# Residual rows of four token tiles loaded ahead of the last product, into the large pool instead of a ring of two

## The chip, the cores and the metric

The kernel runs on one core of a Trainium2 chip. The metric is the device time of one execution in microseconds (us), lower is better. A core has five engines that take instructions in program order, each from its own queue: TensorE (PE), VectorE (DVE), ScalarE (ACT), GpSimd (POOL) and SyncE (SP). SP computes nothing here. It issues nearly all the loads and stores (DMAs), again in program order, and an issue that has to wait holds back everything behind it in SP's queue.

## What is computed

1024 tokens of width 1024, all in float32, pass through two blocks. The three places that the change touches have one shape: a wide hidden activation is multiplied by a "down" matrix and added to the residual row of the token.

```python
# first block
z = rms_norm(h, norm_mlp_g);   h = h + square(relu(z @ w_up)) @ w_down        # way back 1
z = rms_norm(h, norm_ple_g);   h = h + sigmoid(z @ w_ple_gate + b) * (p @ w_ple_proj)
h = rms_norm(h, norm_final_g)
# second block: ffn with a gate, then a mixer, then ffn with a gate
h = h + 0.5 * rms(ffn1(h)) * g1      # ffn(z) = (silu(z @ w_g) * (z @ w_u)) @ w_o    # way back 2
h = h + rms(mixer(h)) * g2
h = h + 0.5 * rms(ffn2(h)) * g3                                                # way back 3
```

## The kernel before

The tokens are cut into eight tiles of 128 rows, t = 0 to 7. A float32 product is made of three matmuls on split operands: ACT rounds an operand to its high half (`wh` of the activation, `tt` of the weight; L687), DVE subtracts to get the low half (`wl`, and the second `tt`; L688), and PE multiplies high by high, high by low and low by high.

`down_s` is the way back. It forms the product with `w_down` (or `f_out`) by seven products of half-size blocks, as Strassen does, in the order 2, 1, 5, 3, 6, 7, 4. Each product is a row of units. A unit loads one piece of the activation from memory (`sd`, from `hs`) and one of the weight (`wd`, from the weight itself, or `td`, a prepared difference), both issued by SP at L660 into tiles of the large pool `u`, of 4 KB a partition. The units of a product are numbered q = 0, 1, and so on. The first way back has the loads `wd`, and DVE subtracts two of them (L669) before the split; the second and third have `td`.

At the end of a product its four PSUM banks are emptied into `Y`, by copies on ACT (L730) or by additions on DVE (L731). After product 7 come four additions for the tiles 4 to 7, and product 4 then finishes these four tiles. For each finished tile `first(t)` is called: it loads the residual row (`xr`, 512 KB, L307) through a pool of two buffers, the ring, and so the loads of the tiles 6 and 7 have to wait until the rows of the tiles 4 and 5 have been used. In the second and third ways back the residual row is used at L1128 (`Y = Y * r + xr`), after a multiplication by the gain (L1121) and after `r`, the reciprocal root that POOL makes of a row's sum of squares (L383, L384). The result goes out by a DMA at L1130, from ACT's queue in way back 2 (to `xb`), from SP's in way back 3 (to `out`). In way back 2 `xs` (L128, ACT) is the normalized tile that PE transposes (L155) for the next projection.

The order of the instructions on each engine is made ahead of time by a scheduler that simulates the program; dependences added by `after` steer it and cost nothing on the chip. "Stage 1, 2 and 3" below are the ends of the three ways back: the last part of product 7, product 4, and what follows until the next product starts. They lie at about 924 to 990 us, 1757 to 1830 us and 2997 to 3054 us.

Of the kernel before, what the change touches and what calls it, by code (L numbers as in the profile page):

```python
# [21 lines left out]
NT = S // P  # L22
# [90 lines left out]
class Z:  # L113
# [5 lines left out]
    def __init__(self, m, gain, whole=False, early=False):  # L119

        self.m, self.gain, self.whole, self.early = m, gain, whole, early
        self.src, self.left = [None] * NT, [0, 1]
        self.tiles = [[], []]
        self.drain = None
# [123 lines left out]
class Model:  # L248
    def __init__(self, ctx, tc, a, out):
        self.tc, self.nc, self.a, self.out = tc, tc.nc, a, out  # L250
        pool = lambda n, b, **k: ctx.enter_context(tc.tile_pool(name=n, bufs=b, **k))
        self.pc = pool("c", 1)
        self.pu = pool("u", 32)
        self.pw = pool("w", NW)
        self.pr = pool("r", 2)
        self.pt = pool("t", 5)
        self.psm = pool("sm", 8)
        self.pd = pool("d", 1, space=DRAM)
        self.last_raw = None
        self.ps = pool("ps", 8, space=PSUM)  # L260


# [363 lines left out]
    def rights(self, w, tw, d):  # L626
# [9 lines left out]
        for i, t in enumerate((x, y)):  # L636
            nc.sync.dma_start(out=tw[d // 2][2 * i : 2 * i + 2, d % 2].rearrange("i p f -> p i f"), in_=t)


    RIGHT = {5: 0, 7: 1, 4: 2, 6: 3}  # L640


    LEFT = {2: (0, 0), 1: (0, 1), 5: (1, 0), 3: (1, 1), 6: (2, 0), 7: (2, 1), 4: (3, 0)}

    def down_s(self, hs, w, Y, done, z=None, aside={}, tail=1, tw=None):

        nc = self.nc
# [4 lines left out]
        ends = [self.late]  # L654
# [36 lines left out]
        def unit(p, q):  # L691
            n = qs[q][1]
            g, i = self.LEFT[p]
            s = load("sd", hs[q][g][i, :n], q)
            return pair(("wh", "wl"), s, n), pair(("u", "u"), right(p, q), n)

        def mm(bank, un, c, t, start, stop):
            (sh, sl), (th, tl) = un
            ts = slice(t * P, (t + 1) * P)
            for k, (x, y) in enumerate(((sh, th), (sh, tl), (sl, th))):  # L700
                self.mark = nc.tensor.matmul(bank, x[:, c, ts], y[:, c], start=start and k == 0, stop=stop and k == 2,  # L701
                                             skip_group_check=True)

        def product(p, banks, start, out, mid=None):
            nq = len(qs)
            head = nq - (tail if p == 4 else 1)
            for q in range(head):
                un = unit(p, q)
                for c in range(qs[q][1]):
                    for t in range(4):  # L710
                        mm(banks[t], un, c, t, start and q == 0 and c == 0, False)
                ends.append(self.mark)
                for f in aside.get((p, q), ()):
                    f()
                if q % 2 and chores:
                    chores.pop(0)()
            uns = [(q, unit(p, q)) for q in range(head, nq)]
            if mid:
                mid()
            for t in range(4):  # L720
                for q, un in uns:
                    for c in range(qs[q][1]):
                        mm(banks[t], un, c, t, start and q == 0 and c == 0, q == nq - 1 and c == qs[q][1] - 1)
                out(t)
            ends.append(self.mark)
# [31 lines left out]
        if z:  # L757
            chores.append(lambda: z.flush(3))
        product(7, a, False, lambda t: plus(4 + t, B, a[t]))

        def rest():
            while chores:
                chores.pop(0)()
            if z:
                z.ready(0)
# [201 lines left out]
    def mlp(self, z, aside={}):  # L967
        nc = self.nc
        hs, xy = [], {}

        def use(n, quarter, bank, other):
            i, j = quarter
            if (n, j) not in xy:
                xy[n, j] = self.u("h", shape=[P, 2, H], tag="s" if (n, j) == (1, 1) else "u")
            o = xy[n, j][:, (1 - i) if j == 0 else i]
            if other is not None:
                nc.vector.tensor_tensor(o, bank, other, op=ALU.add)
                bank = o
            nc.scalar.activation(o, bank, AF.Relu)
            nc.scalar.activation(o, o, AF.Square)  # L980
            if quarter == (1, 0):
                self.lay_by(hs, n, xy.pop((n, 0)), xy.pop((n, 1)), "s")

        self.ups_s(z, use)
        Y = [None] * NT

        def first(t):
            r = self.raw(self.xm[t], name="xr", tag="xr", after=self.mark)
            nc.vector.tensor_tensor(Y[t], Y[t], r, op=ALU.add)
            return self.rstd(Y[t])  # L990

        done, z = self.follow("norm_ple_g", first, lambda t, r: (Y[t], r))
        aside = dict(aside)
        aside[7, 4] = [self.ple_in]
        self.down_s(hs, self.a["w_down"], Y, done, z, aside)
        self.resume()
        return Y, z

# [115 lines left out]
    def seam(self, Y, G, xin, xout, gain, whole=False):  # L1114

        nc = self.nc

        def first(t):
            x = self.raw(xin[t], name="xr", tag="xr", after=self.mark)
            r = self.rstd(Y[t])  # L1120
            nc.vector.tensor_tensor(Y[t], Y[t], G, op=ALU.mult)  # L1121
            return x, r

        def second(t, s):
            if s is None:
                return
            x, r = s
            nc.vector.scalar_tensor_tensor(out=Y[t], in0=Y[t], scalar=r, in1=x, op0=ALU.mult, op1=ALU.add)  # L1128
            r = self.rstd(Y[t]) if gain else None
            (nc.scalar if gain else nc.sync).dma_start(out=xout[t], in_=Y[t])  # L1130
            return r

        if gain:
            return self.follow(gain, first, second, lambda t, r: (Y[t], r), whole=whole)
        state = []

        def done(t):
            state.append(first(t))
            if t:
                second(t - 1, state[t - 1])  # L1140
            if t in (3, NT - 1):
                second(t, state[t])
                state[t] = None

        return done, None

    def ffn(self, n, z, seam, aside={}):
        nc = self.nc
        hs, G, X = [], {}, {}

        def use(p, quarter, bank, other):
            d, up = divmod(p, 2)
            i, j = quarter
            at = (1 - i) if j == 0 else i
            T = X if up else G
            if (d, j) not in T:
                T[d, j] = self.u("h", shape=[P, 2, H]) if up else self.u("g", tag="s", shape=[P, 2, H])
            o = T[d, j][:, at]
            if other is not None:
                nc.vector.tensor_tensor(o, bank, other, op=ALU.add)  # L1160
                bank = o
            if not up:
                nc.scalar.activation(o, bank, AF.Silu)
                return
            nc.vector.tensor_tensor(o, bank, G[d, j][:, at], op=ALU.mult)  # L1165
            if quarter == (1, 0):
                self.lay_by(hs, d, X.pop((d, 0)), X.pop((d, 1)), "u")

        w, tw = self.a["f%d_out" % n], []

        def also(k, of):
            if (k + 1) * w.shape[1] // of > k * w.shape[1] // of:
                self.rights(w, tw, k * w.shape[1] // of)

        self.ups_s(z, use, also)
        Y = [None] * NT
        done, z = seam(Y)
        self.down_s(hs, w, Y, done, z, aside, 1 if z else 2, tw)
        return z

    def half_scale(self, row, name):
# [505 lines left out]
    def block2(self, z, aside):  # L1687
        x0, x1, x2 = self.xd, self.spill("xb"), self.spill("xc")
        rows = [self.out[t * P : (t + 1) * P, :] for t in range(NT)]
        G1 = self.half_scale(2, "g1")  # L1690
        z = self.ffn(1, z, lambda Y: self.seam(Y, G1, x0, x1, "mix_pre_g_2", True), aside)
        self.resume()
        G2 = self.bcast(self.a["rows"][3], "g2")
        z = self.mixer2(z, lambda Y: self.seam(Y, G2, x1, x2, "ffn2_pre_g_2", None))
        G3 = self.half_scale(4, "g3")
        self.ffn(2, z, lambda Y: self.seam(Y, G3, x2, rows, None))

def build(tc, a, out):
    with ExitStack() as ctx:
# [30 lines left out]
```

## Time and profile before

| what | value |
|---|---|
| median of three runs | 3056.68 us (3054.08 to 3061.38) |
| the profiled execution, its own time | 3056.01 us |
| its span in the profile | 3054.2 us |
| PE busy | 2828.5 us (93%) |
| DVE, ACT, POOL busy | 1797.1 us (59%), 1320.1 us (43%), 784.1 us (26%) |
| mean granted clock of PE | 0.968 |
| loads `sd` in all | 126 of 512 KB, median 5.5 us from issue to landing |

The span is the time between the first and the last instruction that the profiler recorded; 1.8 us of the execution's own time lie around it. A share of busy time is a mean over the whole span. What a change in one stage is worth is read from that stage's own waits.

### The profile page before, as it was taken

What the parts mean: (1) busy time and instruction counts of PE and PEld (TensorE: products, weight loads), DVE (VectorE), ACT (ScalarE), POOL (GpSimd) and SP (SyncE); (2) the same over time, 40 slices, a digit from 0 to 9 for tenths busy, and PEclk for the clock granted to TensorE, in tenths of its full rate; (3) what the DMA queues carried; (4) which work ended last, traced back from release to release, by engine and by line L of the source; (5) the groups of instructions that cost most, each with busy time, mean ns of one, the idle gap of its engine ahead of it and who ended that gap; (6) DMA issues with size and microseconds to landing.
All of it is one profiled execution on the core that took longest, in us unless ns stands there. A gap on an engine that the chain in (4) does not pass through costs nothing. (4 is left out here: it accounts for less than half of the span.)

```text
span 3054.2 us, 33886 instructions
## 1 busy us (share of the span) xinstructions
PE 2828.5 (93%) x12585; PEld 2303.4 (75%) x12585; DVE 1797.1 (59%) x2561; ACT 1320.1 (43%) x1921; POOL 784.1 (26%) x626
## 2 busy tenths in 40 slices
PE   8998999989979989999989999997789999998997
PEld 7777877767757867778777878886677778777776
DVE  4586655575767366666667561417735756565445
ACT  5446554442335473323324362236655533332343
POOL 3320222200211221111122041349854112111001
PEclk9999999999989999999999999999899899999999
DMA  4114344474466123454466562423113244446645
GB/s 145 57 47 138 131 145 152 156 259 160 166 233 220 56 90 106 153 164 151 164 222 237 207 222 81 155 83 111 42 49 131 87 152 159 159 153 207 225 160 200
DMA packets 198200, 452.93 MB, mean 148 GB/s; under 512 B 20533, under 2 KB 25233, under 8 KB 198033
## 3 DMA queue, kind: packets, MB, share of 16 engines
q1 hardware_dynamic: 193424, 433.97, 41.9%
q10 hardware_dynamic: 4608, 16.78, 1.4%
q8 instruction: 99, 1.62, 0.2%
q14 instruction: 69, 0.56, 0.1%
HBM read 316.51 MB, written 129.99 MB: 146 GB/s over the span
## 5 line engine op out<-in xcount | busy, mean ns | idle before, releaser
L701 PE MATMUL b<-tt,wh 128*128 128x512 f32 x2128 | 686.2, 403 | 74.0 <-ACT tt L687 64.4
L541 PE MATMUL b<-zh,wh 128*128 128x512 f32 x1680 | 646.9, 398 | 35.4 <-ACT wh L481 25.6
L541 PE MATMUL b<-zh,wl 128*128 128x512 f32 x1680 | 625.3, 393 | 4.5 <-ACT wl L511 4.0
L541 PE MATMUL b<-zl,wh 128*128 128x512 f32 x1560 | 615.2, 395 | 8.4 <-DVE zl L211 8.4
L701 PEld LDWEIGHTS b<-tt,wh 128*128 128x128 f32 x2128 | 409.3, 194 | 181.5 <-ACT tt L687 73.8
L701 PE MATMUL b<-tt,wl 128*128 128x512 f32 x1064 | 424.1, 399 | 0.0
L541 PEld LDWEIGHTS b<-zh,wh 128*128 128x128 f32 x1680 | 319.8, 191 | 123.9 <-ACT wh L481 38.8
L541 PEld LDWEIGHTS b<-zh,wl 128*128 128x128 f32 x1680 | 318.2, 190 | 75.5 <-ACT wl L511 6.7
L541 PEld LDWEIGHTS b<-zl,wh 128*128 128x128 f32 x1560 | 296.4, 190 | 73.9 <-DVE zl L211 13.4
L688 DVE TENSOR_TENSOR wl<-sd,wh 128x1024 fp32r<-128x1024 f32 x140 | 167.6, 1197 | 190.3 <-ACT wh L687 190.3
L482 POOL TENSOR_TENSOR wl<-raw,wh 128x1024 fp32r<-128x1024 f32 x51 | 123.3, 2418 | 526.1 <-ACT wh L481 486.6
L701 PEld LDWEIGHTS b<-tt,wl 128*128 128x128 f32 x1064 | 206.7, 194 | 43.6
L481 ACT ACTIVATE wh<-raw 128x1024 fp32r<-128x1024 f32 x120 | 127.2, 1060 | 238.4 <-DMA raw<-in_f_in 95.2
L352 POOL TENSOR_TENSOR wl<-raw,wh 128x1024 fp32r<-128x1024 f32 (+1 forms) x58 | 142.7, 2465 | 322.0 <-ACT wh L351 290.2
L687 ACT ACTIVATE wh<-sd 128x1024 fp32r<-128x1024 f32 x140 | 141.5, 1011 | 154.6 <-DMA sd<-hs 111.9
L383 POOL TENSOR_SCALAR v<-ss 128x1 f32<-128x1 f32 x80 | 47.9, 599 | 472.5 <-ACT junk L376 466.3
L619 POOL TENSOR_TENSOR hw<-h 128x512 f32<-128x512 f32 x38 | 60.2, 1583 | 421.1 <-DVE h L1165 188.1
L687 ACT ACTIVATE tt<-wd 128x1024 fp32r<-128x1024 f32 x92 | 94.6, 1028 | 150.3 <-DVE wd L669 133.1
L505 DVE TENSOR_TENSOR s<-raw 128x512 f32<-128x512 f32 x60 | 82.2, 1370 | 107.5 <-DMA raw<-in_f_in 100.6
L482 DVE TENSOR_TENSOR wl<-raw,wh 128x1024 fp32r<-128x1024 f32 x69 | 88.7, 1286 | 84.2 <-ACT wh L481 43.2
L351 ACT ACTIVATE wh<-raw 128x1024 fp32r<-128x1024 f32 (+1 forms) x58 | 59.5, 1031 | 168.2 <-issue 42.7
L688 DVE TENSOR_TENSOR tt<-wd,tt 128x1024 fp32r<-128x1024 f32 x92 | 110.2, 1198 | 27.6 <-ACT tt L687 26.8
(358 smaller groups left out, 5003.4 us busy)
## 6 DMA issues: line engine op xcount, KB each, us to landing
sd<-hs SPq DMA_DIRECT2D x126, 512.0 KB, 5.5
raw<-in_f_in SPq DMA_DIRECT2D x94, 512.0 KB, 3.7
wd<-in_w_down SPq DMA_DIRECT2D x64, 512.0 KB, 6.3
raw<-in_f_out SPq DMA_DIRECT2D x44, 512.0 KB, 3.6
tw<-raw SPq DMA_DIRECT2D x44, 512.0 KB, 2.9
td<-tw SPq DMA_DIRECT2D x40, 512.0 KB, 6.3
hs<-h SPq DMA_DIRECT2D x38, 512.0 KB, 3.1
hs<-hw SPq DMA_DIRECT2D x38, 512.0 KB, 3.0
```

The costliest lines, as they stand in the source:

```text
L351: nc.scalar.activation(h, r, AF.Copy)
L352: nc.gpsimd.tensor_tensor(l, r, h.bitcast(F32), op=ALU.subtract)
L383: nc.gpsimd.tensor_scalar(out=v, in0=ss, scalar1=1.0 / D, scalar2=EPS, op0=ALU.mult, op1=ALU.add)
L481: nc.scalar.activation(hi.rearrange("p a b -> p (a b)"), x, AF.Copy)
L482: eng.tensor_tensor(lo.rearrange("p a b -> p (a b)"), x, hi.bitcast(F32).rearrange("p a b -> p (a b)"), op=ALU.subtract)
L505: v.tensor_tensor(s1, a21, a22, op=ALU.add)
L541: self.mark = nc.tensor.matmul(bank, w, x, start=start and k == 0 and i == 0, stop=k == 3 and i == 2, skip_group_check=True)
L619: g.tensor_tensor(wt[:, 1], x[:, 1], y[:, 0], op=ALU.subtract)
L687: nc.scalar.activation(hi[:, :n], x[:, :n], AF.Copy)
L688: v.tensor_tensor(lo[:, :n], x[:, :n], hi.bitcast(F32)[:, :n], op=ALU.subtract)
L701: self.mark = nc.tensor.matmul(bank, x[:, c, ts], y[:, c], start=start and k == 0, stop=stop and k == 2, skip_group_check=True)
```

## The change

After the last addition of product 7 has been emitted, four loads `xe` are issued on SP, one for each residual row of the tiles 4 to 7, into tiles of the pool `u`. `row` then hands these tiles to `first(t)`, and only the tiles 0 to 3 still go through the ring.

```diff
+    def row(self, xin, t):
+        return self.rows.pop(t) if t in self.rows else self.raw(xin[t], name="xr", tag="xr", after=self.mark)
...
         product(7, a, False, lambda t: plus(4 + t, B, a[t]))
+        for t in range(4, NT):
+            x = self.rows[t] = self.u("xe")
+            self.after(nc.sync.dma_start(out=x, in_=xin[t]), ends[-5])
...
         def first(t):
-            r = self.raw(self.xm[t], name="xr", tag="xr", after=self.mark)
+            r = self.row(self.xm, t)
...
         def first(t):
-            x = self.raw(xin[t], name="xr", tag="xr", after=self.mark)
+            x = self.row(xin, t)
```

The lines of the changed kernel have other numbers from there on: L660 becomes L665, L669 L674, L688 L693, L730 L735, L731 L736, L1121 L1129, L1128 L1136, L1130 L1138.

**SP in stage 3.** The queue from the store of tile 1 on, before (the number behind a name is its buffer's; `hs3` is the activation of product 4, unit by unit, and `xc2` the residual row of tile 2):

```order
L1130 DMA out<-Y_21265 128x1024
L660 DMA sd_22351<-hs3_18399 128x2x512
L660 DMA td_22357<-tw_18630 128x2x512
L660 DMA sd_22387<-hs3_18873 128x2x512
L660 DMA td_22393<-tw_19183 128x2x512
L660 DMA sd_22435<-hs3_19436 128x2x512
L660 DMA td_22441<-tw_19599 128x2x512
L307 DMA xr_22423<-xc2_8234 128x1024
```

The same place now:

```order
L1138 DMA out<-Y_21265 128x1024
L767 DMA xe_22351<-xc4_8236 128x1024
L767 DMA xe_22353<-xc5_8237 128x1024
L767 DMA xe_22355<-xc6_8238 128x1024
L767 DMA xe_22357<-xc7_8239 128x1024
L665 DMA sd_22359<-hs3_18399 128x2x512
L665 DMA td_22365<-tw_18630 128x2x512
L665 DMA sd_22395<-hs3_18873 128x2x512
```

The four `xe` stand ahead of the first two loads of product 4, and every later load of product 4 is four places further back. It is the same in stages 1 and 2, where the four stand directly ahead of `sd` and `wd` (`td`) of unit 0 too. In the tail of stage 3 the four `xr` between the stores of the tiles 3 to 7 are gone.

**DVE in stage 1.** The end of product 7 and the start of product 4, before (the first three rows are of the last unit of product 7; L731 are its four additions; `wl`, `wd` and `tt` then are of unit 0 of product 4):

```order
L688 TENSOR_TENSOR wl<-sd,wh 128x1024
L669 TENSOR_TENSOR wd<-wd 128x1024
L688 TENSOR_TENSOR tt<-wd,tt 128x1024
L731 TENSOR_TENSOR Y<-b,Y 128x512
L688 TENSOR_TENSOR wl<-sd,wh 128x1024
L669 TENSOR_TENSOR wd<-wd 128x1024
L731 TENSOR_TENSOR Y<-b,Y 128x512 x2
L688 TENSOR_TENSOR tt<-wd,tt 128x1024
L731 TENSOR_TENSOR Y<-b,Y 128x512
```

The same place now:

```order
L693 TENSOR_TENSOR wl<-sd,wh 128x1024
L674 TENSOR_TENSOR wd<-wd 128x1024
L693 TENSOR_TENSOR tt<-wd,tt 128x1024
L736 TENSOR_TENSOR Y<-b,Y 128x512 x4
L693 TENSOR_TENSOR wl<-sd,wh 128x1024
L674 TENSOR_TENSOR wd<-wd 128x1024
L693 TENSOR_TENSOR tt<-wd,tt 128x1024
```

All four additions now stand ahead of the work for unit 0 of product 4, where three of them stood between or behind it.

**ACT in the tail of stage 2.** From the normalized tile `xs` of tile 2 on, before (L730 are the copies of the four last tiles, L376 a sum of squares, L351 the split of a weight for the next projection):

```order
L128 ACTIVATE xs<-Y,r 128x1024
L730 ACTIVATE Y<-b 128x512 x2
L376 ACTIVATE junk,ss<-Y 128x1024
L351 ACTIVATE wh<-raw 128x1024
L730 ACTIVATE Y<-b 128x512
L128 ACTIVATE xs<-Y,r 128x1024
L730 ACTIVATE Y<-b 128x512
```

The same place now:

```order
L128 ACTIVATE xs<-Y,r 128x1024
L352 ACTIVATE wh<-raw 128x1024
L128 ACTIVATE xs<-Y,r 128x1024
L735 ACTIVATE Y<-b 128x512 x4
L352 ACTIVATE wh<-raw 128x1024
```

The second `xs`, that of tile 3, now stands ahead of the four copies.

## Rows read from the trace of the kernel before

**Rows 1.** The chain that ended last: start, us, what it was.

```profile
3045.18 3.88 DMA xr<-xc
```

**Rows 2.** Timeline, tail of stage 3: start, us, instruction [idle before, releaser].

```profile
3046.09 1.29 DVE L1128 SCALAR_TENSOR_TENSOR Y<-Y,r,xr 128x1024 f32<-128x1024 f32 x1 [0.28 <-DMA xr<-xc]
3049.19 1.28 DVE L1128 SCALAR_TENSOR_TENSOR Y<-Y,r,xr 128x1024 f32<-128x1024 f32 x1 [1.81 <-DMA xr<-xc]
3045.95 0.55 POOL L384 TENSOR_TENSOR r<-v,mh 128x1 f32<-128x1 f32 x1
```

**Rows 3.** Timeline, SP's queue in stage 3: when a DMA was issued.

```profile
2998.11 0.78 SPq L660 DMA_DIRECT2D td<-tw  x1
3000.10 0.57 SPq L660 DMA_DIRECT2D sd<-hs  x1
3001.61 0.46 SPq L307 DMA_DIRECT2D xr<-xc  x1
```

**Rows 4.** DMA issues of Rows 3, same order: KB each, us to landing.

```profile
td<-tw SPq DMA_DIRECT2D x1, 512.0 KB, 5.8
sd<-hs SPq DMA_DIRECT2D x1, 512.0 KB, 9.1
xr<-xc SPq DMA_DIRECT2D x1, 512.0 KB, 10.2
```

**Rows 5.** Timeline, stage 3, ACT, PE and DVE at the start of product 4.

```profile
3003.97 1.06 ACT L687 ACTIVATE tt<-td 128x1024 fp32r<-128x1024 f32 x1
3005.84 1.60 PE L701 MATMUL b<-tt,wh 128*128 128x512 f32 x3
3006.80 1.22 DVE L688 TENSOR_TENSOR tt<-td,tt 128x1024 fp32r<-128x1024 f32 x1
3008.07 0.50 PE L701 MATMUL b<-tt,wh 128*128 128x512 f32 x1 [0.63 <-DVE tt L688]
```

**Rows 6.** Timeline, SP's queue in stage 1: weights of units 0 and 1.

```profile
925.05 0.43 SPq L660 DMA_DIRECT2D wd<-in_w_down  x1
932.25 0.41 SPq L660 DMA_DIRECT2D wd<-in_w_down  x1
```

**Rows 7.** DMA issue of the second of Rows 6: KB, us to landing.

```profile
wd<-in_w_down SPq DMA_DIRECT2D x1, 512.0 KB, 5.1
```

**Rows 8.** Timeline, stage 1, DVE and PE at the start of product 4.

```profile
936.97 1.22 DVE L669 TENSOR_TENSOR wd<-wd 128x1024 f32<-128x1024 f32 x1
938.11 1.28 DVE L731 TENSOR_TENSOR Y<-b,Y 128x512 f32<-128x512 f32 x2
940.51 0.68 DVE L731 TENSOR_TENSOR Y<-b,Y 128x512 f32<-128x512 f32 x1
939.39 0.97 PE L701 MATMUL b<-tt,wh 128*128 128x512 f32 x3 [0.79 <-ACT tt L687]
```

**Rows 9.** Timeline, stage 2, SP's queue and PE at product 4.

```profile
1768.59 0.58 SPq L660 DMA_DIRECT2D td<-tw  x1
1777.43 0.50 PE L701 MATMUL b<-tt,wh 128*128 128x512 f32 x1 [0.64 <-DVE tt L688]
```

**Rows 10.** DMA issue of the first of Rows 9: KB, us to landing.

```profile
td<-tw SPq DMA_DIRECT2D x1, 512.0 KB, 9.9
```

**Rows 11.** Timeline, tail of stage 2: tile 3's xs and the transposes.

```profile
1810.48 1.16 ACT L128 ACTIVATE xs<-Y,r 128x1024 f32<-128x1024 f32 x1
1811.69 5.38 PE L155 MATMUL b<-idn,xs 128*128 128x128 f32 x32 [3.32 <-ACT xs L128]
```

**Rows 12.** Windows: length, busy of five engines (instructions), clock, DMA share, GB/s.

```profile
885.00:890.00 5.00, 4.93 (x22) 3.76 (x21) 2.37 (x4) 1.89 (x5) 0.74 (x2) 1.00 1.02 297
890.00:895.00 5.00, 0.67 (x3) 0.21 (x2) 2.45 (x2) 1.80 (x2) 0.00 (x0) 0.92 0.99 340
895.00:900.00 5.00, 4.64 (x11) 3.67 (x12) 3.59 (x3) 2.51 (x4) 0.00 (x0) 0.50 1.03 407
1778.00:1782.00 4.00, 4.00 (x12) 3.13 (x11) 4.00 (x5) 1.91 (x3) 0.00 (x0) 0.57 1.04 389
```

More of the change, by code (lines that the diff above doesn't have):

```diff
@@ L259, in __init__ @@
         self.last_raw = None
+        self.rows = {}
         self.ps = pool("ps", 8, space=PSUM)
@@ L637, in rights, with down_s @@
             nc.sync.dma_start(out=tw[d // 2][2 * i : 2 * i + 2, d % 2].rearrange("i p f -> p i f"), in_=t)
+    def row(self, xin, t):
+        return self.rows.pop(t) if t in self.rows else self.raw(xin[t], name="xr", tag="xr", after=self.mark)
     RIGHT = {5: 0, 7: 1, 4: 2, 6: 3}
     LEFT = {2: (0, 0), 1: (0, 1), 5: (1, 0), 3: (1, 1), 6: (2, 0), 7: (2, 1), 4: (3, 0)}
-    def down_s(self, hs, w, Y, done, z=None, aside={}, tail=1, tw=None):
+    def down_s(self, hs, w, Y, done, xin, z=None, aside={}, tail=1, tw=None):
         nc = self.nc
@@ L994, in mlp @@
         aside[7, 4] = [self.ple_in]
-        self.down_s(hs, self.a["w_down"], Y, done, z, aside)
+        self.down_s(hs, self.a["w_down"], Y, done, self.xm, z, aside)
         self.resume()
@@ L1145, in seam, with ffn @@
         return done, None
-    def ffn(self, n, z, seam, aside={}):
+    def ffn(self, n, z, xin, seam, aside={}):
         nc = self.nc
@@ L1177, in ffn @@
         done, z = seam(Y)
-        self.down_s(hs, w, Y, done, z, aside, 1 if z else 2, tw)
+        self.down_s(hs, w, Y, done, xin, z, aside, 1 if z else 2, tw)
         return z
@@ L1690, in block2 @@
         G1 = self.half_scale(2, "g1")
-        z = self.ffn(1, z, lambda Y: self.seam(Y, G1, x0, x1, "mix_pre_g_2", True), aside)
+        z = self.ffn(1, z, x0, lambda Y: self.seam(Y, G1, x0, x1, "mix_pre_g_2", True), aside)
         self.resume()
@@ L1695, in block2 @@
         G3 = self.half_scale(4, "g3")
-        self.ffn(2, z, lambda Y: self.seam(Y, G3, x2, rows, None))
+        self.ffn(2, z, x2, lambda Y: self.seam(Y, G3, x2, rows, None))
 def build(tc, a, out):
```

## The prediction

> **What bounds the kernel now.** I began with the shares of busy time: PE is busy for 93% of the span, so the other engines count only where PE waits for them, or after its last matmul. Three places have to be looked at, the ends of the three ways back.
>
> The chain of waits that ended last comes first, since it says what the end of the kernel hangs on. Its longest piece is a residual row on its way, 3.88 us [rows 1]. The timeline of the tail shows what this costs: the last two uses of a residual row stand idle for 0.28 and 1.81 us until their row has landed [rows 2]. That is the wait that the ring of two makes, and the change removes it.
>
> Next I read SP's queue at the start of product 4 in stage 3, with the time that each load took to land. The first `td` landed at 2998.11 + 5.8 = 3003.9, the fifth load at 3000.10 + 9.1 = 3009.2, the `xr` in the seventh place at 3001.61 + 10.2 = 3011.8 [rows 3, 4]. The loads were issued within 4 us, and they landed one behind the other, the later ones 1.3 us apart. So place in SP's queue is time. Then ACT, PE and DVE at the same place: `tt` is split from the moment `td` is there (3003.97), the second half is done by DVE at 3006.80 + 1.22 = 3008.0, and PE, which had done three matmuls on the high half at 3005.84, goes on at 3008.07 [rows 5]. The first loads of product 4 have no slack now: what they lose, PE loses.
>
> **The change in stage 3.** Four loads of 512 KB are put ahead of product 4's first `sd` and `td`. The new `td` stands in the sixth place, and no row has that place; halfway between the fifth and the seventh landing it is 3010.5 [rows 3, 4]. From there the chain is as before: ACT 1.06, so PE can begin on the high half at 3011.6, and DVE 1.22, so the low half is there at 3012.8 [rows 5]. Before it was 3008.0: the rest of product 4 begins 4.7 us later. DVE has its four additions behind it by then and adds nothing. Unit 1 then is in time: its `td`, in the eighth place, lands 1.3 us after the seventh at 3013.1, its low half is there at 3015.4, 3.8 us after PE has begun on unit 0, which keeps PE longer than that. If `td` lands as early as the fifth load did, 3009.2, the start is 3.5 us late; that is the lower bound.
>
> The Trainium skill, "DMA: Bandwidth & Descriptors", section "Anatomy of one DMA — SWDGE (gpsimd) path", gives about 2 us and then the bytes at 436 GB/s for one transfer. By that, as an estimate, four transfers of 512 KB take 4.8 us, `td` lands at 3008.7 and the start is 3.0 us late instead of 4.7; no row here shows this path (the loads are SP's), and the 1.3 us apart are nearer to 1.2 than my 6.6 us for four places.
>
> In the tail of stage 3 the two waits go: 0.28 + 1.81 = 2.1 us [rows 2]. What is late next is DVE itself: without waits the last use begins at 3046.09 - 0.28 + 1.29 = 3047.1, and POOL's last `r` is ready at 3046.50 [rows 2]. If the four stores crowd each other, less remains, 1.3 us at the least.
>
> **The change in stage 1.** Here the first `wd` of product 4 was asked for at 925.05, and in the new order the four `xe` take the places of the loads of units 0 and 1, so that `wd` of unit 0 goes where that of unit 1 went, at 932.25 [rows 6], and lands 5.1 us later, at 937.4 [rows 7]. That alone is harmless, since before DVE came to that `wd` at 936.97. The other half is DVE's queue: the four additions of product 7 now stand together ahead of `wl` and L669 of unit 0. The last of them cannot begin before PE is through with product 7, at 939.39 - 0.79 = 938.6 [rows 8]. An addition takes about 0.7 (two take 1.28), L669 and `wl` 1.22 each [rows 8]: 938.6 + 0.7 + 1.2 + 1.2 = 941.7, then ACT's 1.06 for `tt` [rows 5], so PE begins at 942.8 instead of 939.39, +3.4. If the additions wait for the banks one by one, as the last row of DVE suggests (940.51), it is up to +4.1; I take +3.7. In the tail of stage 1 PE has no wait that a residual row ends, so nothing is gained there.
>
> **The change in stage 2.** The first `xe` goes where the `sd` of unit 0 went, the others follow after the wait that `td` of unit 0 had; `td` of unit 0 comes into the place of the one issued at 1768.59 [rows 9], which took 9.9 us [rows 10] to 1778.5. With ACT's 1.06 and DVE's 1.22 [rows 5] the low half is ready at 1780.8, where PE went on at 1777.43 [rows 9]: +3.4. In the tail `xs` of tile 3 now stands ahead of the four copies on ACT. Before, the 32 transposes waited 3.32 us for it [rows 11], with PE idle. Its inputs are ready long before product 4 ends, so I take the whole 3.3 us as gained; what it may cost is its own 1.16 us [rows 11] ahead of the copies, hence 2.2 at the least.
>
> **The clock.** After it stood still, PE ran at half speed in stage 1 already: after a stretch with 0.67 us busy of 5, 890 to 895, the stretch 895 to 900 has a granted clock of 0.50, half the matmuls of 885 to 890 [rows 12]. That is the lower of the two levels, 1.2 of 2.4 GHz, and costs 5 x 0.5 = 2.5 us. Stages 1 and 3 ran at 1.00 at this place, and will now stand still for 4 to 6 us each: +2.5 each, or nothing, or 3.0 where the low clock lasts a little longer. Stage 2 pays already: a clock of 0.57 in 1778 to 1782 [rows 12] is 4 x 0.43 = 1.7 us; from there to 2.5 is +0.8.
>
> **The sum.** Stage 1: +3.7 + 2.5 = +6.2. Stage 2: +3.4 + 0.8 - 3.3 = +0.9. Stage 3: +4.7 + 2.5 - 2.1 = +5.1. Together +12.2 us against the profiled execution, 3056.0 us: 3068 us. The median of the runs is 0.7 us above that execution, which I leave aside. With every term at its end, no clock loss and least lateness, it is 3.4 + (3.4 - 3.3) + (3.5 - 2.1) = +4.9, 3061 us; with all at the other end (4.1 + 3.0) + (3.4 + 1.3 - 2.2) + (4.7 + 3.0 - 1.3) = +16.0, 3072 us. 3061 to 3072 is the likeliest case's own range.
>
> The SBUF tiles for `xe` cost nothing: they take slots that the loads of unit 0 had waited for at the same places. Their use in place of `xr` changes no instruction's length.
>
> **Rivals.**
> *Late loads, full clock.* PE stands still as I say, but the gap is broken by the first matmuls on the high half, and the clock stays at 1.00, as in stage 3 before, where a wait of 0.63 us [rows 5] took nothing. Then the clock's 5.8 us go and +6.4 remain, 3062 us. Against it: the gaps will be over 4 us, like that of [rows 12].
> *Hidden transfers, shorter tails.* The four `xe` share the engines with product 4's loads without putting them back, or product 7 covers them. It decides whether the new `td` lands by about 3005.7 in stage 3, since PE needs its low half, 2.3 us later, at 3008.0 [rows 5]. Then only the tails count, -2.1 and -3.3, and with the additions in stage 1 in DVE's way for 1 us at most, the sum is -4.4 to -5.4; with the small gaps of the transposes' followers too it may pass -6: 3050 to 3052 us. This case ends faster than before. Against it are the landings one behind the other [rows 4]. The Trainium skill, "DMA: Bandwidth & Descriptors", section "Rules for kernel authors", has the rule for this side: issue the DMA early, compute, wait for it late. The trace agrees for the residual rows themselves (the 1.81 us of [rows 2] are a load issued late), and shows nothing of the loads that are then behind them.
> *Product 4 stays late.* In stage 3 the row of tile 2 (`xr`, the last of [rows 3]) also goes four places back, to about 3017, and DVE stands at its use, ahead of the split of unit 3. If unit 3 or a later unit misses its turn, each stage loses another 2 to 4 us: 3074 to 3078 us. Against it: a unit has 24 matmuls, 22 take 5 us [rows 12], so PE needs unit 3 some 16 us after its start, at 3028.
>
> **How the numbers follow.** Chances: forecast 0.52; late loads at full clock 0.24; hidden transfers 0.14; product 4 stays late 0.10. 0.2% is 6.1 us, about what a measurement of this kernel tells from no change. Slower by more: the forecast but for its low end, 0.44, the third rival 0.10, and little of the first, which stands at the border: 0.55. Within 0.2%: the rest of these and half of the second rival: 0.33. Faster: 0.12, from the second rival and from what the tail of stage 2 may give beyond my 3.3. The range 3052 to 3074 leaves one in ten out on either side.
>
> **What would show it.** In the profile after, four `xe` ahead of `sd` in SP's queue at about 2997.6, the new `td` landing at 3010 or later, and PE waiting 4 to 6 us at the start of product 4 in stages 1 and 3, with a clock of 0.5 to 0.6 behind it; the transposes of stage 2 without the 3.3 us; the last two L1136 without a wait for a DMA. The prediction is wrong if product 4's `td` lands within 6 us of its issue in the new order, if product 7 ends later than I take it, or if the shifted schedule of another stage moves PE's waits by more than these few microseconds.

## The result, and the profile after

The changed kernel is slower. Its median of five runs is 3072.72 us (3069.53 to 3075.64) beside 3056.34 (3052.63 to 3061.38) of before, also five; the ratio is 1.0051, with a 95% interval of 1.0039 to 1.0062, so 12 to 19 us. The profiled execution took 3069.53 us, with a span of 3067.7: 13.5 above that of before.

In stage 3 SP's queue reads like this. Before, the loads of product 4 stood directly behind the store:

```profile
3005.68 0.34 SPq L1138 DMA_DIRECT2D out<-Y  x1
3006.12 2.25 SPq L767 DMA_DIRECT2D xe<-xc  x4
3008.46 0.48 SPq L665 DMA_DIRECT2D sd<-hs  x1
3009.03 0.82 SPq L665 DMA_DIRECT2D td<-tw  x1
```

The four issues take SP 2.25 us, and `td` goes out 3.35 us after the store, where it was 0.92 us [rows 3; the store at 2997.19]. The chain of waits of the changed kernel, cut to this place (start, us, what), leads from that `td` to PE:

```profile
3009.03 9.55 DMA td<-tw
3018.67 1.06 ACT tt L692
3019.78 2.50 PE b L706 x5
```

`td` lands at 3018.6, 12.9 us after its store's issue, where it was 6.7 before (2997.19 to 3003.9). PE waits 5.40 us for the split of it, where its longest wait here was 0.63 us [rows 5]:

```profile
3019.78 2.50 PE L706 MATMUL b<-tt,wh 128*128 128x512 f32 x5 [5.40 <-ACT tt L692]
```

The clock after that wait, in windows of 2 us (columns as in [rows 12]; the number behind the five busy times is the clock):

```profile
3018.00:3020.00 2.00, 0.22 (x1) 0.22 (x2) 1.47 (x2) 1.46 (x2) 0.00 (x0) 0.74 1.03 381
3020.00:3022.00 2.00, 2.00 (x5) 1.60 (x6) 1.87 (x2) 1.68 (x2) 0.00 (x0) 0.50 1.06 391
3022.00:3024.00 2.00, 2.00 (x6) 1.53 (x5) 1.73 (x3) 1.50 (x2) 0.00 (x0) 0.50 1.03 397
3024.00:3026.00 2.00, 2.00 (x6) 1.57 (x6) 1.95 (x2) 1.06 (x1) 0.00 (x0) 0.55 1.04 386
```

PE works for some 6 us at a granted clock of 0.50, the lower of its two levels, and loses 3.0 us by it. In the tail the timeline of DVE shows that no residual row is waited for any more; where the last two uses waited 0.28 and 1.81 us for their rows before [rows 2], what is left is 0.44 us for POOL's `r`:

```profile
3060.70 1.28 DVE L1136 SCALAR_TENSOR_TENSOR Y<-Y,r,xe 128x1024 f32<-128x1024 f32 x1
3062.41 1.28 DVE L1136 SCALAR_TENSOR_TENSOR Y<-Y,r,xe 128x1024 f32<-128x1024 f32 x1 [0.44 <-POOL r L385]
```

In stage 1, SP's queue, DVE and PE at the start of product 4, to be read against [rows 6, 8]:

```profile
925.63 5.93 SPq L767 DMA_DIRECT2D xe<-xm  x4
...
933.24 0.46 SPq L665 DMA_DIRECT2D wd<-in_w_down  x1
...
939.67 0.69 DVE L736 TENSOR_TENSOR Y<-b,Y 128x512 f32<-128x512 f32 x1 [0.44 <-PE b L706]
940.28 1.22 DVE L693 TENSOR_TENSOR wl<-sd,wh 128x1024 fp32r<-128x1024 f32 x1
941.42 1.22 DVE L674 TENSOR_TENSOR wd<-wd 128x1024 f32<-128x1024 f32 x1
...
943.78 0.80 PE L706 MATMUL b<-tt,wh 128*128 128x512 f32 x1 [4.14 <-ACT tt L692]
```

The four additions are through at 940.3, `wl` and L674 come behind them one by one, and PE begins at 943.78 after a wait of 4.14 us, where it waited 0.79. Behind this wait, too, the clock is low, but for a shorter time than in stage 3:

```profile
944.00:946.00 2.00, 2.00 (x5) 1.60 (x6) 2.00 (x2) 0.67 (x1) 0.00 (x0) 0.50 0.90 344
946.00:948.00 2.00, 2.00 (x8) 1.55 (x7) 1.25 (x2) 0.63 (x1) 0.00 (x0) 0.73 0.37 76
```

That takes some 1.6 us.

In stage 2 PE waits 4.51 us at the start of product 4, where it waited 1.24 us for a bank and 0.64 for the low half [rows 9] before. The timeline of PE there, first before and then after:

```profile
1776.30 0.49 PE L701 MATMUL b<-tt,wh 128*128 128x512 f32 x1 [1.24 <-DVE Y L731]
...
1784.35 2.07 PE L706 MATMUL b<-tt,wh 128*128 128x512 f32 x4 [4.51 <-ACT tt L692]
```

In the tail of stage 2 the wait of 3.32 us for the transposes [rows 11] is gone. A longer wait for `zf`, the transposed tile that DVE or ACT copies out of PSUM, is there instead. PE's waits for it from 1764 to 1850 us (us in total, how often, the longest); the first two rows are before, the last is after:

```profile
PE b L428 <- DVE zf L173: 1.2, 2, 0.9
PE b L427 <- ACT zf L172: 0.5, 1, 0.5
...
PE b L428 <- DVE zf L173: 2.4, 1, 2.4
```

To split the 13.5 us, I compare the starts of the same instruction in the two profiles.

| place | before | after | later by |
|---|---|---|---|
| PE's end of product 7, stage 1 (start less wait) | 938.6 | 939.6 | 1.0 |
| ACT's first copy of product 4, stage 1 | 982.20 | 988.46 | 6.3 |
| last matmul of product 7, stage 2 | 1773.56 | 1779.45 | 5.9 |
| first matmul of the attention in block 2 | 2080.06 | 2085.58 | 5.5 |
| last matmul of the attention | 2252.04 | 2260.83 | 8.8 |
| last matmul of product 7, stage 3 | 3005.53 | 3013.99 | 8.5 |
| end of the span | 3054.2 | 3067.7 | 13.5 |

Stage 1 costs 5.3 us, stage 2 gives back 0.4, stage 3 costs 5.0. Another 3.3 us appear in the attention, where no load was moved, and 1.0 us ahead of stage 1; in between 0.7 us are gained. The profiled execution is the fastest of the five; what the median loses beyond 13.5 us is located in no profile.

### The profile page after: what moved, and what is told of

The parts are those of the page before. It is cut to its first block, busy times and chain, and to the rows that moved or that the text cites. A ratio compares the mean times of both kernels' runs of the same rounds, so it can differ in the third digit from the quotient of the medians.

```text
span 3067.7 us, 33882 instructions
## 1 busy us (share of the span) xinstructions
PE 2835.6 (92%) x12585; PEld 2311.4 (75%) x12585; DVE 1794.1 (58%) x2561; ACT 1321.7 (43%) x1921; POOL 789.8 (26%) x626
## 5 line engine op out<-in xcount | busy, mean ns | idle before, releaser
L693 DVE TENSOR_TENSOR wl<-sd,wh 128x1024 fp32r<-128x1024 f32 x140 | 167.5, 1196 | 198.6 <-ACT wh L692 198.2
L693 DVE TENSOR_TENSOR tt<-wd,tt 128x1024 fp32r<-128x1024 f32 x92 | 110.2, 1198 | 29.0 <-ACT tt L692 28.1
```

The lines of the kernel that those rows point to most:

```text
L693: v.tensor_tensor(lo[:, :n], x[:, :n], hi.bitcast(F32)[:, :n], op=ALU.subtract)
```

## The experiments

Theory one is that of the prediction: product 4's first loads are late because four rows go ahead of them. The rivals: the tiles taken out of the large pool, or the missing ring, cost; or the scheduler's new order elsewhere costs; or the transfers are hidden and the loss lies elsewhere. "Stage 3" below is the time from the start of product 7's last matmul to the end of the span, 48.7 us before (3005.53 to 3054.2). "Attention" is the time from its first matmul to its last, 172.0 us before (2080.06 to 2252.04). Ratios are those of the runs of a kernel to the runs of before on the same chip (5 of them for the first row of the changed kernel; 19, 29 and 31 in the three series behind it). The two lengths come from one profile each. An edit is shown against the changed kernel, that of the order alone against the kernel before; `...` marks what is left out.

| kernel | ratio (95%) | attention, us | stage 3, us |
|---|---|---|---|
| before | | 172.0 | 48.7 |
| changed | 1.0051 (1.0039 to 1.0062) | 175.3 | 53.7 |
| changed, again | 1.0049 (1.0035 to 1.0063) | 174.1 | 52.7 |
| stage 1 only | 1.0053 (1.0038 to 1.0068) | 180.1 | 52.1 |
| stage 2 only | 1.0034 (1.0022 to 1.0046) | 176.4 | 49.6 |
| stage 3 only | 1.0011 (0.9999 to 1.0023) | 172.4 | 53.2 |
| late rows | 1.0057 (1.0039 to 1.0075) | 176.4 | 53.1 |
| own tiles | 0.9986 (0.9976 to 0.9996) | 171.6 | 48.0 |
| order only, b | 1.0014 (1.0004 to 1.0025) | 176.7 | 49.5 |
| order only, c | 1.0026 (1.0017 to 1.0035) | 176.9 | 50.5 |
| stage 3, two rows | 0.9998 (0.9986 to 1.0011) | 171.8 | 49.3 |
| stage 3, parts | 0.9999 (0.9989 to 1.0010) | 174.5 | 51.0 |
| stage 3, ACT's queue | 1.0011 (1.0000 to 1.0022) | 171.6 | 53.5 |
| stage 3, PE filled | 1.0009 (0.9999 to 1.0020) | 171.5 | 50.9 |

Three kernels have the same order of instructions in stage 3 and no early row there: before, stage 2 only, and b. Their stage 3 takes 48.7 to 49.6 us, so a difference of 1 us between two profiles says nothing there. The other two without an early row in stage 3 and with the ring, stage 1 only and c, have a new order on DVE and PE there as well, and take 52.1 and 50.5 us.

### One stage at a time

```diff
-        for t in range(4, NT):
+        stage = 1 if tw is None else 2 if z else 3
+        for t in range(4, NT) if stage == 1 else ():     # or 2, or 3
```

> The four early rows in the first way back alone; the other two use the ring of two as before. If the late first loads of product 4 are the cause, stage 1 pays here what it paid with the whole change: PE waits about 4.1 us at the start of product 4, then a low clock, and the end of product 4 is 6 to 7 us late with no gain in the tail: +6 us (+4 to +8). If the loss came from the shifted schedule or from the tiles taken out of the large pool, and not from one place, this third of the change would give about a third of the 16 us, +5 us, but without the 4 us wait at this place.

> The four early rows in the second way back alone. By the late loads: PE waits 4.5 us at the start of product 4 of this stage, the tail gives back the 3.3 us of the transposes, and the sum is about 0 (-2 to +2). If the gain of the tail were not real, or were lost again in the mixer behind it (the whole change was 3 us later there than at the start of it), +3 to +4.

> The four early rows in the third way back alone. By the late loads: a PE wait of 5.4 us, six microseconds at half the clock, less 1.8 us in the tail: +4.7 us (+3 to +6). By a loss that is spread over the kernel: about 0 here, since nothing but the tail is behind this place, or even -2 from the tail.

Stage 3 alone came out as expected: in it 4.5 us, with a wait of 5.11 us and the low clock behind it. The other two are far off. The kernels with stage 1 or 2 alone lose 16 and 10 us by their ratios, more than their stage can. In the profile of the first, PE is 6.2 us later after stage 1 than ahead of it, as expected, and then 8.1 us are lost in the attention. In that of the second, the attention loses 4.4 us, and stage 2 itself misses its expectation: from product 7's last matmul to the attention it takes 310.7 us, 4.2 more than before, where the whole change took 0.4 less. The tail gives nothing back here. The wait for the transposes shrinks to 0.37 us, but the waits for `zf` grow from 1.6 to 6.5 us (timeline of PE, stage 2 alone):

```profile
1810.23 3.71 PE L155 MATMUL b<-idn,xs 128*128 128x128 f32 x32 [0.37 <-ACT xs L128]
...
1818.72 0.61 PE L428 MATMUL b<-zf,wh 128*128 128x512 f32 x1 [4.78 <-DVE zf L173]
...
1822.31 0.79 PE L429 MATMUL b<-zf,wh 128*128 128x512 f32 x1 [1.69 <-DVE zf L173]
```

Three excesses that add up to 0.98% where the whole is 0.51% are not three independent costs. With stage 3 alone, the timeline of PE at the start of its product 4:

```profile
3012.89 2.50 PE L706 MATMUL b<-tt,wh 128*128 128x512 f32 x5 [5.11 <-ACT tt L692]
```

And a window behind that wait:

```profile
3013.00:3015.00 2.00, 2.00 (x5) 1.61 (x6) 1.86 (x2) 1.56 (x2) 0.00 (x0) 0.50 1.04 385
```

It stands at half the clock, as in the whole change.

### The rows behind unit 2

```diff
+                if p == 4 and q == 2:
+                    ask()
...
-        for t in range(4, NT):
-            x = self.rows[t] = self.u("xe")
-            self.after(nc.sync.dma_start(out=x, in_=xin[t]), ends[-5])
+        def ask():
+            for t in range(4, NT):
+                x = self.rows[t] = self.u("xe")
+                self.after(nc.sync.dma_start(out=x, in_=xin[t]), self.mark)
```

> The same four rows, in the same tiles of the large pool, in all three ways back, but asked for after unit 2 of product 4 and not ahead of its first loads. If the place in SP's queue is the cause, the waits at the start of product 4 go back to those of before (0.8, 1.2 and 0.6 us), the tails keep their gains of 3.3 and 1.8 us, and the kernel is 5 us faster than before (-7 to -2). If the tiles of the large pool or the missing ring are the cause, it stays 8 to 16 us slower than before.

This miss was the more useful one. The waits at the start of product 4 did go back, and the time did not. PE now waits inside product 4, for the unit whose loads stand behind the four rows (timeline of PE, stages 1 and 3):

```profile
957.05 1.22 PE L706 MATMUL b<-tt,wh 128*128 128x512 f32 x2 [3.91 <-ACT tt L692]
...
3044.39 2.08 PE L706 MATMUL b<-tt,wh 128*128 128x512 f32 x4 [3.30 <-ACT tt L692]
```

So it is not the start of product 4 that is short of slack; wherever the four rows stand ahead of a load that PE needs soon, that load is what is late. Part of the loss is not these waits: the order in the attention is that of the changed kernel, and 4.4 us are lost there. By itself this run doesn't clear the tiles of the large pool; the next does.

### The rows in their own tiles, at the old place

```diff
     def row(self, xin, t):
-        return self.rows.pop(t) if t in self.rows else self.raw(xin[t], name="xr", tag="xr", after=self.mark)
+        if t < 4 or xin is self.x1:
+            return self.raw(xin[t], name="xr", tag="xr", after=self.mark)
+        x = self.u("xe")
+        self.after(self.nc.sync.dma_start(out=x, in_=xin[t]), self.mark)
+        return x
...
-        for t in range(4, NT):
-            x = self.rows[t] = self.u("xe")
-            self.after(nc.sync.dma_start(out=x, in_=xin[t]), ends[-5])
```

> The four rows of the tiles 4 to 7 in tiles of the large pool, but asked for where they were asked for before, when their tile is finished in the program, and so behind all loads of product 4; no ring of two for them, and the order of the attention is that of the kernel before. If the place ahead of product 4's loads is what costs, nothing waits at the start of product 4 beyond the 0.8, 1.2 and 0.6 us of before, the tail of stage 3 gains the 1.8 us of the ring, that of stage 2 something of its 3.3: -2 to -5 us. If the tiles of the large pool cost, +4 or more.

It is faster than before, by 0.14% (0.04 to 0.24), some 4 us. The rows stand behind the last load of product 4 in SP's queue, and the last use waits as little as in the changed kernel:

```profile
3012.69 0.49 SPq L669 DMA_DIRECT2D td<-tw  x1
3020.40 0.34 SPq L1139 DMA_DIRECT2D out<-Y  x1
3020.84 2.29 SPq L644 DMA_DIRECT2D xe<-xc  x4
...
3042.94 1.28 DVE L1137 SCALAR_TENSOR_TENSOR Y<-Y,r,xe 128x1024 f32<-128x1024 f32 x1 [0.44 <-POOL r L385]
```

(`x1` is the residual of the mixer, which the edit leaves in the ring.) No wait is added at the start of product 4: from 925 to 1000 us PE waits 1.3 us in two pieces for ACT's `tt` and 0.3 for DVE's, as before. The large pool and the missing ring therefore cost nothing here, and most of the change's one gain in stage 3 is to be had without its loss: from the start of PE's last matmul to the end of the span it is 15.6 us, beside 17.0 before and 15.3 in the changed kernel. From product 7 of stage 2 to the attention its profile is 2.6 us shorter than that of before. Not all of that need be the edit's: two kernels whose stage 2 is that of before, the parts and PE filled, are 1.8 and 1.7 us shorter there.

### The order alone

```diff
-            self.after(d, ends[max(len(ends) - ahead, 0)])
+            late = q < 1 and len(ends) > 6 * len(qs) and (tw is None)     # q < 2 for c
+            self.after(d, ends[max(len(ends) - (1 if late else ahead), 0)])
```

> The kernel before, with the ring and no early row. One dependence that exists in the scheduler alone makes the first two loads of product 4 of stage 1 look late to it; SP's order there stays as it was, but far behind, in the attention, the instructions of PE, ACT and DVE come in the order that the kernel with early rows in stage 2 alone has (ACT's and DVE's is that of the changed kernel). If that new order is what costs 3 to 6 us between 2100 and 2300 us in three of the runs, this kernel is 3 to 6 us slower than before, and all of it is there. If those microseconds were differences from one execution to the next, it is within 2 us of before.

> The same with the loads of two units, so that the attention has the order of the kernel with early rows in stage 1 alone, to the last instruction of PE. By the cost of the order: +6 to +10 us, between 2100 and 2300 us. By differences between executions: within 2 us of before.

Both are slower than before, with no row early: by 1 to 8 us and by 5 to 11. The first and last matmul of the attention in the timeline of before:

```profile
2080.06 0.22 PE L1596 MATMUL b<-kd,qq 128*128 128x128 f32 x1
...
2252.04 0.33 PE L1624 MATMUL po<-pl,vv 128*128 128x128 f32 x1
```

In that of c:

```profile
2086.93 0.22 PE L1597 MATMUL b<-kd,qq 128*128 128x128 f32 x1
...
2263.80 0.33 PE L1625 MATMUL po<-pl,vv 128*128 128x128 f32 x1
```

And in that of the changed kernel:

```profile
2085.58 0.22 PE L1604 MATMUL b<-kd,qq 128*128 128x128 f32 x1
...
2260.83 0.33 PE L1632 MATMUL po<-pl,vv 128*128 128x128 f32 x1
```

From first to last it is 176.9 and 175.3 us, beside 172.0 before: a new order without early rows loses at least as much there as the whole change. In the traces c has in the attention, on PE, ACT and DVE, the order of stage 1 alone; b has on ACT and DVE the order of the changed kernel, and on PE that of stage 2 alone. The changed kernel's own order on PE was not run without early rows.

What changed there is which of several ready instructions comes first. An example is ACT's queue in the attention (`ph` is a copy from PSUM, `P` and `den` are the exponentials of the softmax with their sums), before:

```
L1621 ACTIVATE ph_16082<-b_16077 128x512
L1573 ACTIVATE vv_16041<-v_14263 128x8x64
L1602 ACTIVATE P_16044,den_16047<-P_16044,mx_16046 128x128
L1602 ACTIVATE P_16044,den_16047<-P_16044,mx_16046 128x256
L1602 ACTIVATE P_16045,den_16047<-P_16045,mx_16046 128x384
L1602 ACTIVATE P_16045,den_16047<-P_16045,mx_16046 128x512
```

And in the changed kernel, where the same copy stands four places further back:

```
L1581 ACTIVATE vv_16041<-v_14263 128x8x64
L1610 ACTIVATE P_16044,den_16047<-P_16044,mx_16046 128x128
L1610 ACTIVATE P_16044,den_16047<-P_16044,mx_16046 128x256
L1610 ACTIVATE P_16045,den_16047<-P_16045,mx_16046 128x384
L1629 ACTIVATE ph_16082<-b_16077 128x512
L1610 ACTIVATE P_16045,den_16047<-P_16045,mx_16046 128x512
```

Seven kernels here have the attention's order of before: 171.5 to 172.4 us in six profiles, 174.5 in one. Seven profiles are of kernels with a new order: 174.1 to 180.1. By b and c the order is enough for the difference, without the rows. One profile each can't tell the new orders apart, and the two groups overlap at their ends (174.5 and 174.1 us). Not all of b's loss is in the attention: its tail of stage 2 has a wait of 3.2 us for `zf`, where the longest was 0.9 before, so my expectation that "all of it" would be in the attention was wrong.

> The changed kernel once more, beside the three others on one chip, for a second profile and more runs. Its first profile lay 13.5 us above that of before, and the medians 16 apart. By the sum over the stages: stage 1 +6, stage 2 about 0, stage 3 +5, and the attention +3 to +6: 14 to 17 us in all.

15 us by the ratio, as expected. The second profile gives 2.1 us more in the attention than before, and 4.0 in stage 3. Its span is 20.4 us above that of before, and 5.7 of them lie between the attention and stage 3, where the first profile of the same kernel lost nothing.

### What in the four rows is late

```diff
-        for t in range(4, NT):
+        for t in range(6, NT) if not z else ():          # two rows, stage 3 alone
```

> In stage 3 alone, only the rows of the tiles 6 and 7 early; the tiles 4 and 5 use the ring. Read in the profile from the end of product 7 to the end of the kernel, against 5.4 us of waiting with four early rows. If each 512 KB put ahead costs its 1.3 us: the first td lands 2.6 us earlier than with four, PE waits about 2.8 us, the tail keeps its 1.8 us, and the sum for stage 3 is +1 to +3. If four early rows cost by being there at all, 5 us as before.

```diff
-        return self.rows.pop(t) if t in self.rows else self.raw(xin[t], name="xr", tag="xr", after=self.mark)
...
+        x = self.rows.pop(t)
+        self.after(self.nc.sync.dma_start(out=x[:, P:], in_=xin[t][:, P:]), self.mark)
+        return x
...
-        for t in range(4, NT):
+        for t in range(4, NT) if not z else ():
             x = self.rows[t] = self.u("xe")
-            self.after(nc.sync.dma_start(out=x, in_=xin[t]), ends[-5])
+            self.after(nc.sync.dma_start(out=x[:, :P], in_=xin[t][:, :P]), ends[-5])
```

> In stage 3 alone: four early loads at the same place and in the same number, but each of 64 KB (128 of the 1024 columns); the other 896 columns are asked for behind all loads of product 4. If the bytes ahead in the queue cost, the first td is only about 1 us late, PE waits 1 to 2 us, the clock stays up, and stage 3 is at -1 to +1. If the four issues or their places cost, PE waits about 5 us as with whole rows.

```diff
-        for t in range(4, NT):
+        for t in range(4, NT) if not z else ():
             x = self.rows[t] = self.u("xe")
-            self.after(nc.sync.dma_start(out=x, in_=xin[t]), ends[-5])
+            self.after(nc.scalar.dma_start(out=x, in_=xin[t]), ends[-5])
```

> In stage 3 alone, the four whole rows early, but issued by ACT, from its own queue, while SP's queue holds product 4's loads as before. The Trainium skill, DMA: Bandwidth & Descriptors, section Issuing engines are not separate DMA queues, says that they run on the same 16 engines and interleave. If that decides, the first td lands about as late as behind the rows in SP's queue, PE waits 4 to 6 us, +4 to +6 in stage 3. If the place in SP's queue alone decides, td lands as before, PE waits 0.6, and stage 3 gains 2.

With two rows the timeline of PE has a wait of 3.06 us at the start of product 4:

```profile
3009.72 1.76 PE L706 MATMUL b<-tt,wh 128*128 128x512 f32 x5 [3.06 <-ACT tt L692]
```

The window behind it shows no low clock, and the stage takes 49.3 us, no more than the kernels without early rows:

```profile
3011.00:3013.00 2.00, 2.00 (x9) 1.66 (x10) 1.74 (x2) 1.42 (x3) 0.00 (x0) 1.00 1.04 395
```

With parts of rows, the timeline of SP (the store, the four issues, and `td`) and of PE:

```profile
3002.82 0.34 SPq L1142 DMA_DIRECT2D out<-Y  x1
3003.25 2.23 SPq L771 DMA_DIRECT2D xe<-xc  x4
...
3006.05 1.42 SPq L669 DMA_DIRECT2D td<-tw  x1
...
3013.86 1.65 PE L710 MATMUL b<-tt,wh 128*128 128x512 f32 x3 [2.57 <-ACT tt L696]
```

And the window behind PE's wait:

```profile
3014.00:3016.00 2.00, 2.00 (x5) 1.63 (x6) 1.53 (x2) 1.26 (x2) 0.00 (x0) 0.50 1.06 411
```

An eighth of the bytes, and still 2.57 us of waiting and the low clock. I had not counted the issues themselves: four of them hold SP for 2.23 us, so `td` goes out 3.23 us after the store instead of 0.92. It then lands 9.9 us after the store (ACT takes it at 3012.75), against 6.7 before and 12.9 behind whole rows. Both the four issues and the bytes cost.

With the rows in ACT's queue, the timeline of ACT (the four issues), of SP (the store and `td`), of ACT again (the split of `td`) and of PE:

```profile
3000.91 1.77 ACTq L767 DMA_DIRECT2D xe<-xc  x4
...
3001.87 0.34 SPq L1138 DMA_DIRECT2D out<-Y  x1
...
3002.80 1.09 SPq L665 DMA_DIRECT2D td<-tw  x1
...
3014.29 1.06 ACT L692 ACTIVATE tt<-td 128x1024 fp32r<-128x1024 f32 x1 [0.30 <-DMA td<-tw]
...
3015.40 1.22 PE L706 MATMUL b<-tt,wh 128*128 128x512 f32 x2 [5.71 <-ACT tt L692]
```

Here SP issues `td` 0.93 us after the store, as before, and it lands 12.4 us after it all the same: PE waits 5.71 us. The Trainium skill, "DMA: Bandwidth & Descriptors", section "Issuing engines are not separate DMA queues", says that transfers issued by different engines run on the same 16 DMA engines and interleave. The trace agrees: behind rows from ACT's queue `td` lands 12.4 us after the store, behind rows from SP's 12.9. At this place whole rows put `td` off without SP's queue being held up.

```diff
+            if p == 7 and not z:
+                (sh, sl), (th, tl) = uns[-1][1]
+                spare = self.bank()
+                for i in range(24):
+                    nc.tensor.matmul(spare, sh[:, 0, :P], th[:, 0], start=i == 0, stop=i == 23, skip_group_check=True)
...
-        for t in range(4, NT):
+        for t in range(4, NT) if not z else ():
```

> In stage 3 alone, the four whole rows early on SP, and between product 7 and product 4 PE does 24 more matmuls of the last unit's operands into a bank that nobody reads: 5.4 us of work at 0.227 us each, in the time in which PE otherwise waits. If the clock is a cost of its own, product 4 starts as late as with stage 3 alone but at a clock of 1.00, and ends 2.5 to 3 us earlier: stage 3 is +1.5 to +2.5 and not +4.5. If the low clock costs nothing by itself, or falls all the same, +4 to +5.

PE works through the wait on matmuls that nobody reads, and goes on with product 4. In the timeline of PE, the first row is of the matmuls without use (22 of the 24 are in the trace):

```profile
3012.03 5.15 PE L735 MATMUL b<-tt,wh 128*128 128x512 f32 x22
3017.02 1.54 PE L706 MATMUL b<-tt,wh 128*128 128x512 f32 x5
```

The window behind has the full clock:

```profile
3018.00:3020.00 2.00, 2.00 (x9) 1.61 (x9) 1.74 (x3) 1.41 (x3) 0.00 (x0) 1.00 1.05 393
```

Stage 3 takes 50.9 us, where it takes 53.2 with PE idle: 2.3 us less for 24 matmuls more, and 2.2 more than before, within the +1.5 to +2.5 expected. Product 4 begins 0.3 us earlier here after product 7 (5.2 us beside 5.5), so some 2 us are left for the low clock as a cost of its own. This stands on one profile of each kernel; the ratios of the runs, 1.0009 and 1.0011, are too wide to tell 2 us.

## Why the prediction was right, step by step

The forecast was 3068 us with a range of 3052 to 3074, and slower; 3072.72 was measured. It held in its mechanism and in its three stages, and left out a fourth place.

- **Stage 3**, forecast +5.1: measured +5.0 in one profile, +4.0 in the other, +4.5 alone. `td` was to land 13.3 us after the store (2997.19 to 3010.5) and did after 12.9; the start was to be 4.7 us late and PE to wait 4 to 6 us, and it waited 5.40; 2.5 us for the clock, where the windows give 3.0 and the run with PE filled some 2; 2.1 us back in the tail, where 1.6 us of waiting went. What was late next there was POOL's `r` and not DVE, as the text had it. The step from the queue to the landing held for whole rows: asked for from ACT's queue, where SP is not held up, they put `td` off to 12.4 us. It left out the four issues, which with an eighth of the bytes hold `td` back by 2.3 of the 3.2 us that it is late.
- **Stage 1**, forecast +6.2: +5.3, and 6.2 in the run with this stage alone. PE waited 4.14 us where it had waited 0.79, 3.4 more, as the lower of the two figures in the text had it: the last addition began at 939.67, when PE was through with product 7, and `wl`, L674 and ACT's `tt` followed it one by one. The clock cost 1.6 us in this profile, where 2.5 were forecast. In the second profile it cost 2.6, and the stage 6.1.
- **Stage 2**, forecast +0.9: -0.4. Product 4's last matmul came 37.4 us after product 7's, where it had been 34.4: +3.0 for the late start and the clock, where 4.2 were forecast. The 3.3 us of the transposes came back, less a new wait of 2.4 us for `zf` in place of 1.6 in three pieces. The forecast did not have the waits for `zf`, and with stage 2 alone, in another order of instructions, they took all of this gain. That the tail gave something back in the whole change owes something to luck.
- **The sum** of the three stages was +12.2 and is +9.9. The step that failed is one that the text had only among the things that would make it wrong, a shifted schedule that moves PE's waits elsewhere: the sum gave the rest of the kernel nothing. The attention alone lost 3.3 and 2.1 us in the two profiles, and the runs of the order alone show that a new order costs 1 to 11 us without any early row. With the 2.1 to 3.3 us of the attention the forecast would have been 3070 to 3071. The right total owes something to the stages having cost a little less than I said.
- **The rivals.** Hidden transfers: no; `td` landed 12.9 us after the store. Late loads at full clock: not in the changed kernel, with 0.50 behind the waits of stages 1 and 3; it is what two rows do (3.06 us of waiting at a clock of 1.00), while 2.57 us with the parts brought the low clock, so the length of the wait doesn't tell it. Product 4 stays late: PE waited no more in stage 3 after the start of product 4.

What stays open: why one new order of the attention costs 2 us and another 8, since each was profiled once or twice; and why the profile of stage 1 alone loses more there than c, whose order on PE, ACT and DVE is the same there, with no early row (180.1 and 176.9 us).

## What to carry to other kernels

A load asked for early is paid for by the loads behind it: before moving one ahead, look at what stands behind it in the queue and how long that has until it is needed; a place behind the last urgent load gave most of the gain of the tail here and none of the loss. Moving the loads to another engine's queue did not help here: the load behind them landed after 12.4 us instead of 12.9. Where a scheduler sets the order, compare it far from the change as well, and test an order by itself: one that came along unasked cost 1 to 11 us here.

## What the runs showed of the hardware that I had not expected

- The wait's length did not set the clock after it: 2.57 us brought some six microseconds at 0.50, 3.06 us brought none (one profile each).
- 24 matmuls without use kept PE busy through its wait and the clock at 1.00, and the stage was 2.3 us shorter in its profile.
- Four issues of 64 KB put the next load's landing off by 3.2 us, two of 512 KB by 4.0 (`td` at 3008.6, its store at 2997.94), four of 512 KB by 6.2: the delay is far from proportional to the bytes (one profile each).
- Executions of one kernel differ by some microseconds in stretches that have nothing to do with the change. In the two profiles of the changed kernel, the way from the end of the attention to product 7 of stage 3 is 753.2 us in one and 759.2 in the other.
